# Head transposes two slots behind their mix, the gated product held to its place, and the pooling maps moved between the products

## The chip, the core and the metric

The kernel runs on one core of a Trainium2 chip. The metric is the device time of one execution in microseconds (us); lower is better. The engines are named as the profile names them: PE (TensorE) multiplies matrices, PEld is its weight load, DVE (VectorE) and ACT (ScalarE) and POOL (GpSimd) work on elements, SP (SyncE) issues the loads.

## What is computed

One block with 512 positions and 1024 channels, all in float32. Cut to what the change touches:

```python
hn = rms_norm(h, g_mix_pre)
z_sgu, z_conv, z_pool, z_gate = split(hn @ w_in)

# A) spatial gating: 8 heads of 128 channels, blocks of 128 positions
u, v = split(gelu(z_sgu)); v = layer_norm(v)
mixed = einsum('hij,bnjhc->bnihc', mask(w_s), v.reshape(blocks)) + b_s
br_a = (u * mixed) @ w_sgu_out

# C) pooling: four groups of 256 channels, windows 2, 4, 8, 16
for g, w in enumerate(windows):
    pooled[g] = trailing_mean(z_pool[g], w) - z_pool[g]
br_c = (einsum('bsgc,gcd->bsgd', pooled, w_pool) * s_pool) @ w_pool_out

merged = gate_a * br_a + gate_b * br_b + gate_c * br_c   # gates = sigmoid(z_gate)
h = h + rms_norm(merged @ w_out)
```

Branch B (a causal depthwise convolution of width 31, LayerNorm, swish), the feed-forward part and an embedding come beside and behind it; the change leaves them as they are.

## The kernel before

Activations lie transposed: channels on the 128 partitions, the 512 positions free, in eight tiles. A float32 product is three passes of a rounded type (high by high, high by low, low by high), so one tile of 128 outputs is 24 matmuls of 128 x 512. I call these 24 matmuls a **product**. Weights come in order of use: SP loads `raw`, ACT casts it to `hi`, DVE subtracts to get `lo`, two products ahead (`AHEAD = 2`).

A scheduler fixes the order of instructions on each engine when the program is built. Instructions issued inside `with order():` stay behind all those written before them on their engine. `drain(n)` issues n taps of the depthwise convolution (`acc` steps) on DVE, in order, behind each product.

In the **gating branch**, `natural` makes u with the positions on partitions, in two halves `c` of four slots `kk`, each of 24 matmuls into `ps_nat`. During the second half `mix_head(h)` splits v, multiplies it into `ps_mix` (3 matmuls), and DVE makes `gated[h]` from it and u. `turn_head(h)` transposes `gated[h]` into `ps_tr` (4 small matmuls), and ACT and DVE split the result into `sgu`. The loop turns head kk - 1 in slot kk and then mixes head kk; heads 3 to 7 follow behind the first gate products (`ps_gate`).

In the **pooling branch** eight products `ps_z` are copied by ACT to `z_all`, two for each of the groups 0 to 3. `pool_windows(g)` makes trailing sums of 2, 4, 8, 16 by doubling on POOL (`win`; 1 to 4 additions, each with a small copy), finishes them on DVE (`win` again), casts them on ACT to `pl_hi` and subtracts on DVE to `pl_lo`. `pool_map(g)` multiplies these by `w_pool` into `ps_pool` (12 matmuls), and ACT and DVE split the result into `pool`. The map of a group stands in the source behind the products of the next group; that of group 3 stands behind the third gate product (`POOL_LAG - 1` is 2).

`psum` has seven banks, handed out in turn, so a matmul into a new tile also waits until the bank's last reader is done. All engine instructions but POOL's carry L69, the line of a helper; what an instruction does is read from its tiles.

Of the kernel before, what the change touches and what calls it, by code (L numbers as in the profile page):

```python
# [13 lines left out]
ALU = mybir.AluOpType  # L14
# [7 lines left out]
NB = T // P  # L22
# [16 lines left out]

# The first GLU pairs are multiplied before the norm of x is known.  # L40
N_RAW = 3
N_FIRST = 2 * N_RAW * P
# Matrix products on nothing that raise the tensor engine's clock while the first loads run.
N_WARM = 8
# Taps of the depthwise convolution for each tile of GLU, v, gate a, pooling, gate c; and of u.
TAPS = (4, 3, 5, 3, 5)
TAPS_U = 4
# Where a norm or a piece of a residual goes between the products, counted in k-tiles.
STAT_K, STAT_A, STAT_H, STAT_F = 4, 2, 7, 2
# [5 lines left out]
class InOrder:  # L55
    """Engines whose instructions, while `on`, are issued behind all those written before them."""

# [24 lines left out]
def hybrid_block(  # L82
# [3 lines left out]
):  # L86
    """Activations live transposed (channels on partitions, the 512 positions free), so that every
    weight is a stationary operand as it lies in memory and is loaded once. A float32 product is
    three float32r passes: each operand is split exactly into a high and a low half of 12 bits."""
    nc = tc.nc  # L90
# [25 lines left out]

# [1 line left out]
    vec = const.tile([P, N_VEC + WIDTH * KT], F32, name="vec")  # L118
# [41 lines left out]

# [1 line left out]
    def split(hi, lo, src):  # L162
# [3 lines left out]
    def split_scaled(hi, lo, src, scale):  # L166
        """The halves of src * scale, scale one number per partition."""
        act_e.activation(out=hi, in_=src, func=AF.Copy, scale=scale)
        dve.scalar_tensor_tensor(out=lo, in0=src, scalar=scale, in1=hi,
                                       op0=ALU.mult, op1=ALU.subtract)  # L170
# [44 lines left out]
    def product(ps, w, acts, hs=FULL, k0=0, last=True):  # L215
        """ps[n, t] (+)= sum over the block's k of w[k, n] act[k, t]."""
        hi, lo = w
        for i, a in enumerate(acts):
            mm3(ps[:, hs], blk(hi, i), blk(lo, i), a[:, 0, hs], a[:, 1, hs],
                k0 + i == 0, last and i == len(acts) - 1)  # L220
# [7 lines left out]

# [1 line left out]
    background = []  # L230
# [6 lines left out]
    def rsqrt(y, a, t):  # L237
        """y = 1 / sqrt(a): a bit-pattern guess, a Newton step scaled by S, a third-order step."""
        dve.tensor_scalar(out=y.bitcast(I32), in0=a.bitcast(I32), scalar1=-0.5,
                          scalar2=RSQRT_SEED, op0=ALU.mult, op1=ALU.add)  # L240
        dve.tensor_tensor(out=t, in0=y, in1=y, op=ALU.mult)
        dve.scalar_tensor_tensor(out=t, in0=t, scalar=-RSQRT_C2 * RSQRT_S, in1=a,
                                 op0=ALU.mult, op1=ALU.mult)
        dve.scalar_tensor_tensor(out=y, in0=t, scalar=RSQRT_C1 * RSQRT_S, in1=y,
                                 op0=ALU.add, op1=ALU.mult)
        dve.tensor_tensor(out=t, in0=y, in1=y, op=ALU.mult)
        dve.tensor_tensor(out=t, in0=t, in1=a, op=ALU.mult)
        dve.scalar_tensor_tensor(out=t, in0=t, scalar=-10.0 / 3.0 * RSQRT_S ** 2, in1=t,
                                 op0=ALU.add, op1=ALU.mult)
        dve.scalar_tensor_tensor(out=y, in0=t, scalar=5.0 * RSQRT_S ** 4, in1=y,  # L250
                                 op0=ALU.add, op1=ALU.mult)

    def channel_mean(sums):
        """The mean over the channels of what `sums` holds by partition, on every partition."""
        ps = psum.tile([P, T], F32, tag="pst", name="ps_stat", bufs=1)
        ps = ps[:, :sums.shape[1]]
        pe.matmul(ps, lhsT=mean_mat, rhs=sums, start=True, stop=True)
        return ps

    def inv_rms(sums, y):  # L260
        """y = 1 / sqrt(mean over the channels + eps), on every partition; eps is in the sums."""
        rsqrt(y, channel_mean(sums), t2("rs_t", sums.shape[1]))
# [6 lines left out]
    def add_square(sums, src, i, engine):  # L269
        """The i-th of the squares that are summed; the second brings eps along."""  # L270
        if i == 0:
            act_e.activation(out=sums, in_=src, func=AF.Square)
        else:
            add_sq(sums, square(src), i, engine)
# [7 lines left out]

# [1 line left out]
    C_U, C_V, C_A, C_G, C_P, C_M = 0, 8, 16, 24, 32, 40  # L284
# [19 lines left out]
    for g in GROUPS:  # L304
        add_mix(C_P + 2 * g, C_P + 2 * g + 1)
        if g != GROUPS[0]:
            weights.add(w_pool[g - 1])
    POOL_LAG = 3
    for n in range(KT + POOL_LAG):
        if n < KT:  # L310
            add_mix(C_M + 16 + n)
        if n == POOL_LAG - 1:
            weights.add(w_pool[GROUPS[-1]])
        if n >= POOL_LAG:
            add_mix(S_POOL + n - POOL_LAG)
# [25 lines left out]

# [1 line left out]
    xg = [slot("br", f"xg{k}") for k in range(KT)]  # L343
# [15 lines left out]

# [1 line left out]
    h_conv = [slot("cv", f"h_conv{i}", F32) for i in range(4)]  # L361
# [67 lines left out]

# [1 line left out]
    def natural(dst, evacuate, taps):  # L431
        """dst[t, block, c] from z with the positions on partitions; yields behind each block."""
        for c in range(2):
# [69 lines left out]
    def mix_head(h):  # L503
        cs = slice(h * P, (h + 1) * P)
        vs = slot("tm", "v_split", shape=(2, NB, P))
        split(vs[:, 0], vs[:, 1], v_all[:, :, cs])
        ps = bank("ps_mix")
        mm3(ps, sg_hi[:, cs], sg_lo[:, cs], vs[:, 0], vs[:, 1], True, True)
        gated[h] = t2("gated")
        dve.scalar_tensor_tensor(  # L510
            out=gated[h].rearrange("p (n c) -> p n c", n=NB), in0=ps.rearrange("p (n c) -> p n c", n=NB),
            scalar=col("b_sgu_s", h), in1=u_all[:, :, cs], op0=ALU.add, op1=ALU.mult)

# [8 lines left out]
    for c, kk in natural(u_all, u_gelu, TAPS_U):  # L522
        if c == 1:
            if kk:
                turn_head(kk - 1)
            mix_head(kk)

# [1 line left out]
    merged = wide_tile("merged")  # L529
# [13 lines left out]
    for n in range(KT + SGU_LAG):  # L543
        if n < KT:
            gate_tile(merged[:, n, :], TAPS[2])
        if n < SGU_LAG:
            for h in ((3,), (4,), (5, 6), (7,))[n]:
                turn_head(h)
# [6 lines left out]

# [1 line left out]
    z_all = wide_tile("z_all")  # L557
# [34 lines left out]
    for g in GROUPS:  # L592
        for n in (2 * g, 2 * g + 1):
            ps = bank("ps_z")
            product(ps, weights.get(), hn)
            act_e.copy(z_all[:, n, :], ps)
            drain(TAPS[3])
        pool_windows(g)
        if g != GROUPS[0]:
            pool_map(g - 1)  # L600

    gates = []
    for n in range(KT + POOL_LAG):
        if n < KT:
            gates.append(t2("gate"))
            gate_tile(gates[n], TAPS[4])
        if n == POOL_LAG - 1:
            pool_map(GROUPS[-1])
        if n >= POOL_LAG:
# [5 lines left out]

# [1 line left out]
    drain(len(background))  # L617
# [31 lines left out]

    # ---- output projection, post-norm, residual; the last tiles a half of the positions at a time,  # L650
    # so that the norm of one half runs behind the product of the other ----
    o_all = wide_tile("o_all")
# [4 lines left out]
    class Residual:  # L657
        """h += o * y tile by tile, and the halves of h * scale; the low half runs a tile behind."""

# [49 lines left out]
    with order():  # L709
# [23 lines left out]

# [1 line left out]
        banks = [bank("ps_f") for _ in range(2 * N_PAIR)]  # L735
# [92 lines left out]
    with order():  # L828
# [26 lines left out]

# [1 line left out]
        w_ple_1 = weights.get(0)  # L857
# [31 lines left out]
def _blocks(w):  # L889
    """[K, N] -> [N / 128, 128, K]: one block for each 128 outputs, its k-tiles side by side."""  # L890
    k, n = w.shape
    return w.reshape(k // P, P, n // P, P).transpose(2, 1, 0, 3).reshape(n // P, P, k)


def _wide_blocks(w):
    """[1024, 1024] -> [8, 128, 1024]: for each half of the outputs, pairs of k-tiles."""
    return w.reshape(4, 2, P, 2, T).transpose(3, 0, 2, 1, 4).reshape(8, P, D)
# [54 lines left out]
```

## Time and profile before

| what | value |
|---|---|
| median of 3 runs | 987.28 us (987.15 to 988.0) |
| span of the profiled execution, first to last instruction | 984.9 us |
| so outside the span, by the median | about 2.4 us |
| PE busy | 974.1 us, 99% of the span |
| DVE busy | 675.5 us, 69% |
| ACT busy | 347.1 us, 35% |
| POOL busy | 87.4 us, 9% |
| granted TensorE clock | 1.000 over the span |

The profile is of one execution, whose own device time is not listed; the span is taken to lie 2.4 us below the median. In the timeline a row gives the start in us from the span's start, the duration, the engine, the operation with its tiles, the number of instructions merged into the row and, in brackets, how long the engine stood idle before it and whose end ended that. A DVE row ends about 0.09 us behind the start of the next, and a 128 x 512 matmul is listed with 0.39 us though the next starts 0.23 us after it. In the text a **step** is the time from one start to the next.

### The profile page before, as it was taken

The page shows a single profiled execution, that of the slowest core. Times are in us where ns is not written, and L with a number is a line of the kernel's source. Part 1 is how long each engine was busy: PE and PEld are TensorE (multiplying, and loading weights), DVE is VectorE, ACT ScalarE, POOL GpSimd, SP SyncE. Part 2 cuts the span into 40 slices and gives each one's busy share as a digit, 9 for nine tenths or more (in the row PEclk, how much of TensorE's full clock was granted, in tenths as well). Part 3 has the DMA queues.
Part 4 walks back from the last instruction along what each step waited for, and adds up shares of the span by engine and source line. Part 5 has one row for each costly group of instructions (what it writes and reads, how often), then busy time and mean ns, then how long its engine had stood idle before and what let it go on. Part 6 is the DMA issues. An engine that isn't in the chain of part 4 may idle for free.

```text
span 984.9 us, 11718 instructions
## 1 busy us (share of the span) xinstructions
PE 974.1 (99%) x4682; PEld 818.4 (83%) x4682; DVE 675.5 (69%) x903; ACT 347.1 (35%) x483; POOL 87.4 (9%) x64
## 2 busy tenths in 40 slices
PE   9999999899999999999999999999999999999998
PEld 6788888688888788888888998888888888888897
DVE  7998789998988799967556687554445442223675
ACT  6422333332223332246426443332232322223442
POOL 4000004000003702160000010000000000000000
PEclk9999999999999999999999999999999999999999
DMA  6433331322222232231328102323222333334312
GB/s 226 143 107 107 109 106 65 106 69 103 86 97 86 76 128 86 102 113 65 116 99 277 65 25 74 116 86 107 88 105 87 104 84 107 93 92 141 107 43 86
DMA packets 30006, 100.53 MB, mean 102 GB/s; under 512 B 3456, under 2 KB 3968, under 8 KB 29952
## 3 DMA queue, kind: packets, MB, share of 16 engines
q1 hardware_dynamic: 29808, 99.75, 30.2%
q8 instruction: 36, 0.59, 0.2%
q14 instruction: 18, 0.15, 0.0%
q10 hardware_dynamic: 144, 0.04, 0.0%
HBM read 97.68 MB, written 2.10 MB: 101 GB/s over the span
## 4 chain that ended last, share of the span: by engine, by line
PE 89%; DVE 7%; issue 2%; DMA 1%; ACT 1%; SPq 0%; DVEq 0%; ACTq 0%
PE ps_f L69 24%; PE ps_gate L69 13%; PE ps_br L69 13%; PE ps_fo L69 12%; PE ps_ag L69 5%; PE ps_pg L69 5%; PE ps_o L69 5%; PE ps_nat L69 4%; PE ps_z L69 4%; DVE lo L69 2%; DVE acc L69 1%; PE ps_pool L69 1%; PE ps_ple L69 1%; DVE v_all L69 1%; DMA first_all<-in_w_first 1%
## 5 line engine op out<-in xcount | busy, mean ns | idle before, releaser
L69 ACT CAST hi<-raw 128x1024 fp32r<-128x1024 f32 (+3 forms) x158 | 162.5, 1030 | 455.6 <-PE ps_br L69 88.4
L69 DVE TENSOR_TENSOR lo<-raw,hi 128x1024 fp32r<-128x1024 f32 (+3 forms) x158 | 201.4, 1276 | 107.5 <-ACT hi L69 106.8
L69 DVE SCALAR_TENSOR_TENSOR acc<-h_conv,vec,acc 128x511 f32<-128x511 f32 (+14 forms) x240 | 184.2, 768 | 5.1
L69 PE MATMUL ps_f<-hg,hi 128*128 128x512 f32 (+1 forms) x624 | 184.3, 378 | 0.0
L69 PEld LDWEIGHTS ps_f<-hg,hi 128*128 128x128 f32 x624 | 115.1, 188 | 21.7
L69 PE MATMUL ps_gate<-hn,hi 128*128 128x512 f32 x384 | 119.4, 392 | 0.0
L69 PE MATMUL ps_f<-hg,lo 128*128 128x512 f32 (+1 forms) x312 | 117.8, 378 | 0.0
L69 PE MATMUL ps_fo<-f,hi 128*128 128x512 f32 (+1 forms) x396 | 110.9, 366 | 0.0
L69 PEld LDWEIGHTS ps_gate<-hn,hi 128*128 128x128 f32 x384 | 72.0, 188 | 15.9 <-issue 1.0
L69 PEld LDWEIGHTS ps_fo<-f,hi 128*128 128x128 f32 x396 | 71.7, 189 | 12.2
L69 PE MATMUL ps_nat<-hi,hn 128*128 128x512 f32 x256 | 79.0, 389 | 0.0
L69 PE MATMUL ps_gate<-hn,lo 128*128 128x512 f32 x192 | 74.8, 389 | 0.0
L69 PE MATMUL ps_fo<-f,lo 128*128 128x512 f32 (+1 forms) x198 | 72.3, 365 | 0.0
L69 PEld LDWEIGHTS ps_f<-hg,lo 128*128 128x128 f32 x312 | 58.7, 188 | 11.0
L69 PEld LDWEIGHTS ps_nat<-hi,hn 128*128 128x128 f32 x256 | 48.1, 188 | 10.0
L69 DVE TENSOR_TENSOR f<-ps_f,h_inv 128x512 f32<-128x512 f32 x22 | 15.2, 689 | 56.5 <-PE ps_f L69 56.5
L69 PE MATMUL ps_nat<-lo,hn 128*128 128x512 f32 x128 | 49.8, 389 | 0.0
L69 PE MATMUL ps_ag<-hn,hi 128*128 128x512 f32 x160 | 49.5, 390 | 0.2 <-DVE sig L69 0.2
L69 PEld LDWEIGHTS ps_gate<-hn,lo 128*128 128x128 f32 x192 | 36.1, 188 | 7.6
L69 PEld LDWEIGHTS ps_fo<-f,lo 128*128 128x128 f32 x198 | 37.3, 189 | 6.0
L69 DVE TENSOR_TENSOR silu<-ps_f,h_inv 128x512 f32<-128x512 f32 x22 | 15.2, 690 | 36.0 <-PE ps_f L69 35.9
L69 PE MATMUL ps_br<-pool,hi 128*128 128x512 f32 x128 | 39.6, 389 | 0.0
(214 smaller groups left out, 1566.1 us busy)
## 6 DMA issues: line engine op xcount, KB each, us to landing
raw<-in_w_mix SPq DMA_DIRECT2D x90, 512.0 KB, 3.2
raw<-in_w_ffn_in SPq DMA_DIRECT2D x44, 512.0 KB, 3.2
raw<-in_w_ffn_out SPq DMA_DIRECT2D x16, 448.0 KB, 3.2
raw<-in_w_ffn_out SPq DMA_DIRECT2D x8, 512.0 KB, 3.5
raw<-in_w_ple_gate SPq DMA_DIRECT2D x8, 512.0 KB, 4.1
x_all<-in_xT SPq DMA_DIRECT2D x8, 256.0 KB, 6.6
h_all<-in_xT SPq DMA_DIRECT2D x4, 512.0 KB, 5.4
out_dram<-pg SPq DMA_DIRECT2D x7, 256.0 KB, 2.0
```

What stands on the lines that cost most here:

```text
L69: inst = op(*args, **kw)
```

## The change

Three things. In the gating branch, a head is turned two slots behind its mix: slot kk turns head kk - 2, and head 2 joins head 3 behind the first gate product. The `gated` step is put inside `with order():`, so it stands in DVE's queue where it is written. In the pooling branch `pool_map` moves: the maps of groups 0 and 1 stand behind the first product of the group after next, those of groups 2 and 3 behind the first and the second gate product. The list of weights follows.

```diff
     for g in GROUPS:
-        add_mix(C_P + 2 * g, C_P + 2 * g + 1)
-        if g != GROUPS[0]:
-            weights.add(w_pool[g - 1])
+        add_mix(C_P + 2 * g)
+        if g > 1:
+            weights.add(w_pool[g - 2])
+        add_mix(C_P + 2 * g + 1)
...
-        if n == POOL_LAG - 1:
-            weights.add(w_pool[GROUPS[-1]])
+        if n < 2:
+            weights.add(w_pool[2 + n])
...
-        dve.scalar_tensor_tensor(
-            out=gated[h].rearrange("p (n c) -> p n c", n=NB), in0=ps.rearrange("p (n c) -> p n c", n=NB),
-            scalar=col("b_sgu_s", h), in1=u_all[:, :, cs], op0=ALU.add, op1=ALU.mult)
+        with order():
+            dve.scalar_tensor_tensor(
+                out=gated[h].rearrange("p (n c) -> p n c", n=NB),
+                in0=ps.rearrange("p (n c) -> p n c", n=NB),
+                scalar=col("b_sgu_s", h), in1=u_all[:, :, cs], op0=ALU.add, op1=ALU.mult)
...
         if c == 1:
-            if kk:
-                turn_head(kk - 1)
+            if kk > 1:
+                turn_head(kk - 2)
             mix_head(kk)
...
-            for h in ((3,), (4,), (5, 6), (7,))[n]:
+            for h in ((2, 3), (4,), (5, 6), (7,))[n]:
                 turn_head(h)
...
             drain(TAPS[3])
+            if g > 1 and n == 2 * g:
+                pool_map(g - 2)
         pool_windows(g)
-        if g != GROUPS[0]:
-            pool_map(g - 1)
...
             gate_tile(gates[n], TAPS[4])
-        if n == POOL_LAG - 1:
-            pool_map(GROUPS[-1])
+        if n < 2:
+            pool_map(2 + n)
```

On PE, at the end of slot kk = 1 of u's second half (its matmuls read `hn_229` and `hn_230`, those of slot 2 `hn_231` onwards), there stood before:

```order
L69 MATMUL ps_nat<-hi,hn_230 128x512 x2
L69 MATMUL ps_nat<-lo,hn_230 128x512
L69 MATMUL ps_tr<-ident,gated 128x128 x4
L69 MATMUL ps_mix<-v_split,w_hi 128x512 x2
L69 MATMUL ps_mix<-v_split,w_lo 128x512
L69 MATMUL ps_nat<-hi,hn_231 128x512 x2
```

and now:

```order
L69 MATMUL ps_nat<-hi,hn_230 128x512 x2
L69 MATMUL ps_nat<-lo,hn_230 128x512
L69 MATMUL ps_mix<-v_split,w_hi 128x512 x2
L69 MATMUL ps_mix<-v_split,w_lo 128x512
L69 MATMUL ps_nat<-hi,hn_231 128x512 x2
```

The transpose of head 0 has gone to the end of slot 2, with the mix of head 2 behind it; those of heads 2 and 3 stand together behind the first gate product. On DVE the `gated` step of head 1 has gone ahead of a `lo` that it followed, and that of head 2 directly behind the next `lo`, ahead of an `sgu` step.

On DVE, between the low half of group 2 (`pl_lo`) and the finishing step of group 3 (`win<-win,z_all 128x2x496`), there stood before:

```order
L69 TENSOR_TENSOR pl_lo<-win,pl_hi 128x1024
L69 TENSOR_TENSOR lo<-raw,hi 128x1024
L69 SCALAR_TENSOR_TENSOR pool_2554<-ps_pool,vec,pool_2554 128x512
L69 TENSOR_TENSOR lo<-raw,hi 128x1024
L69 TENSOR_SCALAR acc_226<-h_conv_222,vec 128x512
L69 SCALAR_TENSOR_TENSOR pool_2564<-ps_pool,vec,pool_2564 128x512
L69 TENSOR_TENSOR lo<-raw,hi 128x512
L69 SCALAR_TENSOR_TENSOR acc_226<-h_conv_222,vec,acc_226 128x511
L69 SCALAR_TENSOR_TENSOR win<-win,z_all 128x2x496
```

and now, behind the same `pl_lo` and the same first `lo`:

```order
L69 TENSOR_SCALAR acc_226<-h_conv_222,vec 128x512
L69 SCALAR_TENSOR_TENSOR acc_226<-h_conv_222,vec,acc_226 128x511
L69 SCALAR_TENSOR_TENSOR acc_226<-h_conv_222,vec,acc_226 128x510
L69 SCALAR_TENSOR_TENSOR acc_226<-h_conv_222,vec,acc_226 128x509
L69 TENSOR_TENSOR lo<-raw,hi 128x512
L69 SCALAR_TENSOR_TENSOR acc_226<-h_conv_222,vec,acc_226 128x508
L69 SCALAR_TENSOR_TENSOR pool_2592<-ps_pool,vec,pool_2592 128x512
L69 TENSOR_TENSOR lo<-raw,hi 128x1024
L69 SCALAR_TENSOR_TENSOR acc_226<-h_conv_222,vec,acc_226 128x507
L69 SCALAR_TENSOR_TENSOR pool_2602<-ps_pool,vec,pool_2602 128x512
L69 SCALAR_TENSOR_TENSOR acc_226<-h_conv_222,vec,acc_226 128x506
L69 SCALAR_TENSOR_TENSOR win<-win,z_all 128x2x496
```

Five more `acc` steps stand ahead of group 3's `win`, and five stand ahead of the first step that waits for `ps_pool`, where there was none.

On ACT, from the copy of the last `ps_z` to the cast of group 3's `pl_hi`, there stood before (a `gate` row is the sigmoid behind a gate product; the third one follows the last row):

```order
L69 COPY z_all<-ps_z 128x512
L69 ACTIVATE pool_2554<-ps_pool,vec 128x512
L69 CAST hi<-raw 128x1024
L69 ACTIVATE pool_2564<-ps_pool,vec 128x512
L69 CAST hi<-raw 128x512
L69 ACTIVATE gate<-ps_gate 128x512
L69 CAST hi<-raw 128x1024
L69 ACTIVATE gate<-ps_gate 128x512
L69 CAST pl_hi<-win 128x1024
L69 CAST hi<-raw 128x1024
```

and now:

```order
L69 COPY z_all<-ps_z 128x512
L69 CAST hi<-raw 128x512
L69 ACTIVATE gate<-ps_gate 128x512
L69 ACTIVATE pool_2592<-ps_pool,vec 128x512
L69 CAST hi<-raw 128x1024
L69 ACTIVATE pool_2602<-ps_pool,vec 128x512
L69 CAST hi<-raw 128x1024
L69 ACTIVATE gate<-ps_gate 128x512
L69 CAST pl_hi<-win 128x1024
L69 CAST hi<-raw 128x1024
```

The cast of `pl_hi` stands behind the second gate's sigmoid in both. On PE the two matmuls `ps_pool<-pl_hi,hi` of group 3 stood directly behind the third gate product, and now directly behind the second.

## Rows read from the trace of the kernel before

**Rows 1.** The page's first part: busy time, share and instructions of each engine.

```profile
PE 974.1 (99%) x4682; PEld 818.4 (83%) x4682; DVE 675.5 (69%) x903; ACT 347.1 (35%) x483; POOL 87.4 (9%) x64
```

**Rows 2.** Waits of PE: what waited, for what, us in total, times, longest.

```profile
PE ps_tr L69 <- DVE gated L69: 3.2, 2, 1.6
...
PE ps_pool L69 <- ACT pl_hi L69: 1.0, 1, 1.0
```

**Rows 3.** Timeline of PE around the head transposes.

```profile
173.24 0.39 PE L69 MATMUL ps_nat<-lo,hn 128*128 128x512 f32 x1
175.19 0.66 PE L69 MATMUL ps_tr<-ident,gated 128*128 128x128 f32 x4 [1.56 <-DVE gated L69]
...
176.37 0.62 PE L69 MATMUL ps_nat<-hi,hn 128*128 128x512 f32 x2
...
190.18 0.66 PE L69 MATMUL ps_tr<-ident,gated 128*128 128x128 f32 x4 [1.59 <-DVE gated L69]
```

**Rows 4.** Timeline of DVE in the same stretch.

```profile
174.39 0.75 DVE L69 SCALAR_TENSOR_TENSOR gated<-ps_mix,vec,u_all 128x512 f32<-128x512 f32 x1
175.05 0.73 DVE L69 SCALAR_TENSOR_TENSOR acc<-h_conv,vec,acc 128x502 f32<-128x502 f32 x1
175.70 1.22 DVE L69 TENSOR_TENSOR lo<-raw,hi 128x1024 fp32r<-128x1024 f32 x1
176.84 0.69 DVE L69 TENSOR_TENSOR v_split<-v_all,v_split 128x512 fp32r<-128x512 f32 x1
177.44 3.06 DVE L69 SCALAR_TENSOR_TENSOR acc<-h_conv,vec,acc 128x501 f32<-128x501 f32 x4
180.41 1.22 DVE L69 TENSOR_TENSOR lo<-raw,hi 128x1024 fp32r<-128x1024 f32 x1
181.55 0.75 DVE L69 SCALAR_TENSOR_TENSOR gated<-ps_mix,vec,u_all 128x512 f32<-128x512 f32 x1
```

**Rows 5.** Timeline of PE around the maps of groups 2 and 3.

```profile
332.27 0.39 PE L69 MATMUL ps_z<-hn,lo 128*128 128x512 f32 x1
333.62 0.73 PE L69 MATMUL ps_pool<-pl_hi,hi 128*128 128x512 f32 x2 [0.97 <-ACT pl_hi L69]
...
352.80 0.62 PE L69 MATMUL ps_pool<-pl_hi,hi 128*128 128x512 f32 x2
```

**Rows 6.** Timeline of ACT in that stretch.

```profile
332.52 1.04 ACT L69 CAST pl_hi<-win 128x1024 fp32r<-128x1024 f32 x1 [3.96 <-DVE win L69]
333.47 1.04 ACT L69 CAST hi<-raw 128x1024 fp32r<-128x1024 f32 x1
334.42 0.58 ACT L69 COPY z_all<-ps_z 128x512 f32<-128x512 f32 x1
...
348.29 0.59 ACT L69 ACTIVATE gate<-ps_gate 128x512 f32<-128x512 f32 x1
350.27 1.05 ACT L69 CAST pl_hi<-win 128x1024 fp32r<-128x1024 f32 x1 [1.39 <-DVE win L69]
```

**Rows 7.** Timeline of DVE in that stretch.

```profile
333.60 1.93 DVE L69 TENSOR_TENSOR pl_lo<-win,pl_hi 128x1024 fp32r<-128x1024 f32 x1 [0.52 <-ACT pl_hi L69]
335.46 2.91 DVE L69 TENSOR_TENSOR lo<-raw,hi 128x1024 fp32r<-128x1024 f32 x1
341.26 0.75 DVE L69 SCALAR_TENSOR_TENSOR pool<-ps_pool,vec,pool 128x512 fp32r<-128x512 f32 x1 [2.89 <-ACT pool L69]
...
348.13 1.18 DVE L69 SCALAR_TENSOR_TENSOR win<-win,z_all 128x992 f32<-128x992 f32 x1
```

**Rows 8.** Timeline of POOL in that stretch: two additions of group 3.

```profile
338.49 1.89 POOL L567 TENSOR_TENSOR win<-win 128x1020 f32<-128x1020 f32 x1
...
342.69 3.32 POOL L567 TENSOR_TENSOR win<-win 128x1008 f32<-128x1008 f32 x1
```

**Rows 9.** Timeline of PE: its first row.

```profile
1.33 3.60 PE L69 MATMUL ps_warm<-warm_up 128*128 128x512 bf16 x8 [1.33 <-DVE warm_up L69]
```

**Rows 10.** The page's part on DMA issues: KB each, us to landing.

```profile
raw<-in_w_mix SPq DMA_DIRECT2D x90, 512.0 KB, 3.2
```

## Prediction

> **What bounds the kernel now.** The page's first part comes first: TensorE is busy for 974.1 us, 99% of the span, VectorE for 675.5 [rows 1]. A change that leaves the matmuls as they are can win only what TensorE waits, and lose by making it wait. So the view of PE's waits is next: head transposes waited for `gated` twice, 3.2 us, and a pooling map once for `pl_hi`, 1.0 [rows 2]. The timeline of PE says where: 1.56 at 175.19 and 1.59 at 190.18 [rows 3], 0.97 at 333.62 [rows 5]. A matmul counts there for 0.39 while the next starts 0.23 behind it, so each wait costs 0.16 more than its bracket: 1.72, 1.75 and 1.13, together 4.6. That is all the change can remove. The timeline of DVE shows why `gated` is late: VectorE has no gap between 174.39 and 181.55, taps and weight halves stand around the step [rows 4].
>
> **The gating branch.** I walk on with steps of VectorE: `gated` 0.66, `acc` 0.65, `lo` 1.14, `v_split` 0.60 (`sgu` has its shape), four `acc` 2.97 [rows 4]. Up to `gated` of head 0 (174.39, done 175.14) nothing differs. TensorE ends slot 1 at 173.47 [rows 3], and now goes on with a mix (3 x 0.23 = 0.68) and slot 2 (24 x 0.227 = 5.44): 179.59. Head 0's transposes find their input done, so the 1.72 goes. Transposes and mix take 1.18 (175.19 to 176.37) [rows 3], slot 3 runs from 180.77 to 186.21, transposes and mix to 187.39.
>
> The first gate product takes the bank of head 2's mix, so it waits for `gated` of head 2. VectorE: from 180.41 `gated` 0.66, `lo` 1.14, `acc` 0.65, `v_split` 0.60, four `acc` 2.97, `lo` 1.14 bring 187.57, and 0.75 more its end, 188.32. TensorE waits for about **0.95**, new, and ends the gate product at about 193.8. Head 2's transposes follow (0.4), then head 3's, whose `gated` stands behind `sgu` 0.60, `acc` 0.65, `v_split` 0.60, three `acc` 2.2, `lo` 1.14 and `acc` 0.65 after the previous one: 188.23 + 5.84 = 194.07, done 194.82. TensorE is there at 194.2 and waits for **0.6**, new. The 1.75 at 190.18 is gone. Behind VectorE's queue stand the same splits as before, and its work is the same, only in another order. Sum: -1.72 - 1.75 + 0.95 + 0.6, **-1.9**. Bounds: -3.5 if neither new wait comes, 0 if VectorE's queue runs 2 late.
>
> The view of PE's waits names nothing else between 191 and 332 [rows 2], so I carry the 1.9 to the last `ps_z`: it ends at 332.50 [rows 5] and now at 330.6.
>
> **The pooling maps.** Maps 0 and 1 move behind one more product and were not waited for: 0. Map 2 goes behind the first gate product, 5.44 later, while it was 1.13 late: **-1.1**, with over 4 to spare. The four loads of `w_pool` move by one or two places in SP's queue. A load lands in 3.2 [rows 10] and is issued two products, 10.9, ahead, so I take 0; without that cover it would be at most 3.2.
>
> Map 3 moves the other way. It stood behind the third gate product and now stands behind the second, one gate product earlier. Before, its matmuls started at 352.80, and `pl_hi` had been done at 351.32 [rows 5, 6]: 1.5 of slack. Now TensorE comes to it two gate products and one map (12 x 0.227 = 2.72) behind the last `ps_z`: 330.6 + 5.44 + 2.72 + 5.44 = 344.2. What it needs: `pl_hi` of group 2 on ACT (332.52), behind it in ACT's queue a `hi` and the copy of the last `ps_z` (334.42), four additions on POOL, `win` on VectorE (348.13), `pl_hi` of group 3 (350.27, done 351.32) [rows 6, 7]. If that chain moves ahead by the 1.9 and keeps its length, it ends at 349.4, and the new wait is **5.2**.
>
> I expect it longer. The rows show that VectorE and POOL stop each other: the `lo` at 335.46 took 2.91 where the same step takes 1.22, and the POOL addition at 342.69 took 3.32 where 338.49's took 1.89 [rows 4, 7, 8]. In the kernel before, POOL had a free stretch, because VectorE stood idle for 2.89 until 341.26, waiting for map 2's `ps_pool` [rows 7]. The order now has five `acc` steps in that place. VectorE's own work from `pl_lo` of group 2 to `win` of group 3 is `pl_lo` and two `lo` 3 x 1.14, seven `acc` steps 7 x 0.65, a short `lo` 0.60 and two `pool` 2 x 0.66: 9.9. POOL's is four additions with their copies, two of which took 338.49 to 342.69, so 8.4 [rows 8]. In full turns, with only `pool` beside POOL (its source is in PSUM, and I take that as free): 9.9 - 1.3 + 8.4 = 17.0, where it was 348.13 - 333.60 = 14.5 [rows 7]. That lengthens the chain by 2.4, and the wait to **7.6**. Ends: 2.5 if the two never meet, since ACT still has to do a `hi` (0.95), the second gate's sigmoid (0.5) and `pl_hi` (1.05) behind that gate product [rows 6]; 9.1 if group 2's three additions are stretched too, which delays the copy that starts group 3. I take 7.6, as the order leaves VectorE no gap.
>
> The Trainium skill, page "SBUF — State Buffer", section "Who interferes with whom", has a rule for this: a VectorE instruction with two SBUF inputs and a GpSimd instruction that reads SBUF exclude each other, and the one that comes later blocks for the other's whole length. This trace agrees with it (2.91 against 1.22). By that rule the wait is the 7.6; by the busy times alone it would be 2.5.
>
> **After the stall.** TensorE would stand idle longer than anywhere in this trace, where 1.6 is the longest [rows 2] and no slower matmuls follow. At its start, after idling, eight matmuls took 3.60 [rows 9], 0.45 each where 0.227 is usual, so at the lower of its two clocks, 1.2 GHz (the granted clock reads 1.000 over the span, so I go by the matmuls). Bounds: 0, as after 1.6, and 1.8 (8 x 0.22), as at the start; twice that if it lasts longer. A wait of 7.6 is nearer to the start than to 1.6, so I take **+1.8**.
>
> The Trainium skill, page "TensorE: Matmul & The Clock Gate", section "Part 1: The HAM clock gate (the "warmup" mystery)", says that an idle array falls to 1.2 GHz and that sustained work brings 2.4 back. The trace shows the second half at its start; no wait in it is long enough for the first.
>
> **The sum.** -1.9 - 1.1 + 7.6 + 1.8 = +6.4. The span of 984.9 becomes 991.3; what lies outside it (2.4) stays, so the median of 987.28 becomes **993.7**.
>
> **Rivals.**
> 1. *The chain keeps its length.* Wait 5.2, for which speaks that the chain before had turns too; against it, the order without the idle 2.89. 987.28 - 3.0 + 5.2 = 989.5, and 991.3 with the slow matmuls.
> 2. *No turns.* Only ACT's order holds, wait 2.5: 986.8, no change to be told. Against it speak the 2.91 and 3.32.
> 3. *Faster: map 3 is not waited for.* The place is the same, the price of the wait 0, the total 984.3. It decides where the chain from the last `ps_z` to `pl_hi` shrinks from 18.8 (332.50 to 351.32) to under 14.6, so that less than 1.0 of wait stands against the 3.0 won. Against it: the sigmoid ahead of `pl_hi` on ACT waits for the second gate product, which alone costs 2.5.
> 4. *Worse:* all three effects at their ends, wait 9.1 and slow matmuls for twice as long: 987.28 - 3.0 + 9.1 + 3.6 = 997.0.
>
> **How the numbers follow.** A measurement here can tell 0.2%, 2.0 us, from no change. The forecast (turns, with or without slow matmuls, 992 to 995.5) has 0.55, rival 1 0.20, rival 2 0.12, rival 3 0.06, rival 4 0.07. Rivals 2 and 3 and part of 4 are left out: 988.5 to 996.5. Within the forecast alone it is 992 to 995.5. Faster (below 985.3) 0.06; same (985.3 to 989.3) 0.15, rival 2 and the lower edge of rival 1; slower 0.79.
>
> **What would show it.** In the changed profile: no wait at the transposes of head 0 and at the end of slot 3; a wait of about 1 at the first `ps_gate` and of 0.6 at head 3's `ps_tr`, both for `gated`; none at map 2; one of 7 to 8 at `ps_pool` for `pl_hi` around 344, with POOL's four additions stretched beyond 11 us and no idle on VectorE among them; then matmuls 0.45 apart. A wait near 5 there says rival 1, near 2.5 rival 2. The prediction is wrong if map 3 is reached late or its cast comes early, and if the two new waits for `gated` are as long as those they replace.

## The result and the profile after

The changed kernel takes 994.23 us (median of 4 runs, 993.77 to 996.14), the kernel before 987.21: ratio 1.0072, 95% interval 1.0058 to 1.0086, so 7.0 us slower. 993.7 was forecast, in 988.5 to 996.5. The profiled execution has a span of 992.4, 7.5 more than before.

The waits of PE after the change (what waited, for what, us in total, times, longest), the answer to [rows 2]:

```profile
PE ps_pool L69 <- ACT pl_hi L69: 7.9, 1, 7.9
...
PE ps_gate L69 <- DVE gated L69: 0.9, 1, 0.9
...
PE ps_tr L69 <- DVE gated L69: 0.4, 1, 0.4
```

The two waits of 1.6 at `ps_tr` are gone, and two shorter ones stand in their place. At `ps_pool` one wait of 7.9 stands where 1.0 stood. The timeline of PE has the places, as [rows 3] and [rows 5] had them before:

```profile
179.78 0.60 PE L69 MATMUL ps_tr<-ident,gated 128*128 128x128 f32 x4
...
188.54 0.73 PE L69 MATMUL ps_gate<-hn,hi 128*128 128x512 f32 x2 [0.86 <-DVE gated L69]
...
195.08 0.63 PE L69 MATMUL ps_tr<-ident,gated 128*128 128x128 f32 x4 [0.36 <-DVE gated L69]
...
352.42 1.22 PE L69 MATMUL ps_pool<-pl_hi,hi 128*128 128x512 f32 x2 [7.91 <-ACT pl_hi L69]
353.44 1.05 PE L69 MATMUL ps_gate<-hn,hi 128*128 128x512 f32 x2
354.29 0.63 PE L69 MATMUL ps_gate<-hn,lo 128*128 128x512 f32 x1
```

Head 0 is transposed without a wait, the first gate product waits for head 2's bank, head 3's transposes wait for their `gated`. The large wait is that of map 3. Behind it two matmuls of a gate take 1.05, where 0.62 is usual [rows 3]; from start to start that is 0.43 for each (353.44 to 354.29).

Why `pl_hi` came so late is read on ACT, POOL and VectorE. ACT, against [rows 6]:

```profile
331.75 1.05 ACT L69 CAST pl_hi<-win 128x1024 fp32r<-128x1024 f32 x1 [5.22 <-DVE win L69]
...
333.65 0.58 ACT L69 COPY z_all<-ps_z 128x512 f32<-128x512 f32 x1
...
345.27 0.59 ACT L69 ACTIVATE gate<-ps_gate 128x512 f32<-128x512 f32 x1
351.32 1.04 ACT L69 CAST pl_hi<-win 128x1024 fp32r<-128x1024 f32 x1 [5.46 <-DVE win L69]
```

The cast of group 3 starts at 351.32, behind 5.46 of idle that ended with `win`; the sigmoid ahead of it had been done since 345.86. So ACT's order, the floor of 2.5, was not what held it. VectorE, against [rows 7]:

```profile
332.84 1.23 DVE L69 TENSOR_TENSOR pl_lo<-win,pl_hi 128x1024 fp32r<-128x1024 f32 x1 [1.20 <-ACT pl_hi L69]
...
335.11 2.12 DVE L69 TENSOR_SCALAR acc<-h_conv,vec 128x512 f32<-128x512 f32 x1
337.26 3.83 DVE L69 SCALAR_TENSOR_TENSOR acc<-h_conv,vec,acc 128x511 f32<-128x511 f32 x3
341.01 2.37 DVE L69 TENSOR_TENSOR lo<-raw,hi 128x512 fp32r<-128x512 f32 x1
...
344.63 2.67 DVE L69 TENSOR_TENSOR lo<-raw,hi 128x1024 fp32r<-128x1024 f32 x1
...
349.19 1.18 DVE L69 SCALAR_TENSOR_TENSOR win<-win,z_all 128x992 f32<-128x992 f32 x1
```

and POOL, against [rows 8]:

```profile
334.31 2.63 POOL L570 TENSOR_TENSOR win<-z_all 128x1022 f32<-128x1022 f32 x1 [1.38 <-ACT z_all L69]
...
337.35 2.41 POOL L570 TENSOR_TENSOR win<-win 128x1020 f32<-128x1020 f32 x1
...
340.44 2.40 POOL L570 TENSOR_TENSOR win<-win 128x1016 f32<-128x1016 f32 x1
...
343.51 2.70 POOL L570 TENSOR_TENSOR win<-win 128x1008 f32<-128x1008 f32 x1
346.16 1.19 POOL L571 COPY win<-win 128x16 f32<-128x16 f32 x1
```

The first addition of group 3 and the copy behind the last one were, before the change:

```profile
335.08 2.20 POOL L567 TENSOR_TENSOR win<-z_all 128x1022 f32<-128x1022 f32 x1 [0.63 <-ACT z_all L69]
...
345.95 0.39 POOL L568 COPY win<-win 128x16 f32<-128x16 f32 x1
```

VectorE has no idle between 332.84 and 349.19, and four of the rows shown are far over their bare length: a `lo` of 1.22 takes 2.67, three taps 3.83 for 2.2. The rows not shown there keep theirs. POOL's additions, 1.89 each when alone [rows 8], take 2.40 to 2.70. From `pl_lo` of group 2 to `win` of group 3 it is 16.35, where it was 14.53. Nearly all of these 1.8 lies on POOL: from its first addition to the end of its last copy it takes 13.04, and 11.26 before.

The windows around the stall (length, busy time of PE, PEld, DVE, ACT, POOL, then the granted clock, the share of the DMA engines and GB/s):

```profile
343.00:346.00 3.00, 1.51 (x7) 0.93 (x5) 3.00 (x4) 1.54 (x2) 2.92 (x2) 1.00 0.51 152
346.00:350.00 4.00, 0.00 (x0) 0.00 (x0) 4.00 (x5) 0.00 (x0) 1.36 (x2) 0.64 0.41 147
350.00:352.00 2.00, 0.00 (x0) 0.00 (x0) 2.00 (x5) 0.68 (x1) 0.00 (x0) 0.50 0.01 2
352.00:354.00 2.00, 1.58 (x4) 1.29 (x5) 2.00 (x3) 0.37 (x1) 0.00 (x0) 0.50 0.35 92
354.00:356.00 2.00, 2.00 (x7) 1.52 (x6) 0.81 (x2) 0.00 (x0) 0.00 (x0) 0.50 0.45 174
356.00:358.00 2.00, 2.00 (x7) 1.61 (x6) 0.00 (x0) 0.00 (x0) 0.00 (x0) 0.65 0.01 4
358.00:360.00 2.00, 2.00 (x10) 1.65 (x9) 0.00 (x0) 0.00 (x0) 0.00 (x0) 1.00 0.00 0
```

The granted clock falls to 0.50 (1.2 GHz) while PE idles and is back at 1.00 (2.4 GHz) from 358. In between the windows count 7 matmuls of PE in 2 us, and 10 from 358.

To put each change of time in its place, I cut every profile at three starts on PE: the first `ps_nat`, the first `ps_br` that reads `sgu`, and the first `ps_o` that reads `mix` at full width. The gating branch lies in the second column, the pooling branch in the third.

| kernel | first `ps_nat` at | to first `ps_br` | to first `ps_o` | to the end | span |
|---|---|---|---|---|---|
| before | 96.1 | 127.6 | 291.4 | 469.8 | 984.9 |
| the change | 96.3 | 125.6 | 300.7 | 469.8 | 992.4 |
| gating branch alone | 96.9 | 125.6 | 291.3 | 469.9 | 983.7 |
| pooling branch alone | 96.8 | 127.6 | 301.1 | 469.8 | 995.3 |
| map 3 behind the third gate | 97.7 | 125.6 | 293.7 | 469.8 | 986.8 |
| map 3 behind the fourth gate | 96.5 | 125.5 | 291.2 | 469.8 | 983.0 |
| stall filled | 96.6 | 125.5 | 298.4 | 469.8 | 990.3 |
| taps behind the map | 96.6 | 125.6 | 297.5 | 469.8 | 989.5 |
| gating alone, fewer taps | 96.1 | 123.8 | 291.4 | 469.8 | 981.1 |
| the best version | 97.0 | 123.8 | 290.6 | 469.8 | 981.2 |

The change wins 2.0 in the gating branch and loses 9.3 in the pooling branch. The first column moves by up to 1.6 between executions; that is the start, which no kernel here changes.

### The profile page after: what moved, and what is told of

Same layout as the page of the kernel before. It is cut to its first block, busy times and chain, and to the rows that moved or that the text cites. A ratio compares the mean times of both kernels' runs of the same rounds, so it can differ in the third digit from the quotient of the medians.

```text
span 992.4 us, 11720 instructions
## 1 busy us (share of the span) xinstructions
PE 976.7 (98%) x4682; PEld 820.5 (83%) x4682; DVE 682.1 (69%) x903; ACT 346.8 (35%) x483; POOL 91.0 (9%) x64
## 4 chain that ended last, share of the span: by engine, by line
PE 88%; DVE 7%; ACT 2%; issue 1%; DMA 1%; SPq 0%; DVEq 0%; ACTq 0%
PE ps_f L69 24%; PE ps_br L69 13%; PE ps_fo L69 12%; PE ps_gate L69 12%; PE ps_nat L69 6%; PE ps_ag L69 5%; PE ps_pg L69 5%; PE ps_o L69 5%; PE ps_z L69 4%; DVE lo L69 2%; DVE acc L69 1%; PE ps_ple L69 1%; PE ps_pool L69 1%; DVE v_all L69 1%; DMA x_all<-in_xT 1%
## 5 line engine op out<-in xcount | busy, mean ns | idle before, releaser
L69 DVE TENSOR_TENSOR lo<-raw,hi 128x1024 fp32r<-128x1024 f32 (+3 forms) x158 | 204.5, 1295 | 112.9 <-ACT hi L69 112.5
L69 DVE SCALAR_TENSOR_TENSOR acc<-h_conv,vec,acc 128x511 f32<-128x511 f32 (+14 forms) x240 | 190.1, 792 | 5.1
L69 PE MATMUL ps_br<-sgu,hi 128*128 128x512 f32 x128 | 39.4, 389 | 0.0
```

Source lines behind the costliest of these rows:

```text
L69: inst = op(*args, **kw)
```

## The experiments

My theory: map 3 comes one gate product too early for a chain (group 2's cast, the copy behind it, POOL, VectorE, the cast) that the same edit has lengthened, since taps now stand where POOL ran free; and the idle time lowers TensorE's clock. Rivals: the gating edit brings TensorE there too early; the place of the map alone, with a chain no longer than before; another cause for the slow matmuls.

**Gating branch alone.** The pooling hunks of the diff are left out.

> Only the gating branch is changed (transposes two slots behind, gated held to its place); the pooling branch is as before. My theory: the two waits of 1.72 and 1.75 go, two new ones of about 1.0 and 0.5 come, so -1.9 us: about 985.3, ratio 0.998. Rival: the new waits are as long as the old, ratio 1.000.

984.92, ratio 0.9974 (0.9964 to 0.9984). The waits of PE:

```profile
PE ps_pool L69 <- ACT pl_hi L69: 1.0, 1, 1.0
PE ps_gate L69 <- DVE gated L69: 0.9, 1, 0.9
...
PE ps_tr L69 <- DVE gated L69: 0.4, 1, 0.4
```

The new waits are shorter than the old, and the stage is 2.0 shorter. Map 2's wait of 1.0 stays, since that is the pooling edit's. Of the three parts of the change one did nothing: with the `with order():` around `gated` taken out, the order on all five engines is the same row by row.

**Pooling branch alone.** The gating hunks are left out.

> Only the pooling branch is changed; the gating branch is as before. My theory: the chain to the last group's pl_hi starts from the pooling products, so it moves with TensorE, and the wait stays at 7.9 whatever the gating branch does; with the wait of 1.1 at map 2 gone and 2.4 for slow matmuls: 987.2 - 1.1 + 8.1 + 2.4 = 996.6, ratio 1.0095. Rival: TensorE only comes too early because the gating edit has moved it up by 1.9; then the wait is 6.0 and the time about 992.7.

996.55, ratio 1.0090 (1.0076 to 1.0104), and PE's waits are

```profile
PE ps_pool L69 <- ACT pl_hi L69: 7.9, 1, 7.9
PE ps_tr L69 <- DVE gated L69: 3.2, 2, 1.6
```

The wait is the same 7.9 without the gating edit. That rival falls: the chain starts from products of TensorE, and moves with it. What the gating branch wins it keeps.

**Map 3 behind the third gate product again.**

```diff
+    POOL_AT = {0: 2, 2: 3}
...
-        if n < 2:
-            pool_map(2 + n)
+        if n in POOL_AT:
+            pool_map(POOL_AT[n])
```

> The whole change, but the map of group 3 stands again behind the third gate product. My theory: TensorE comes 5.44 later, at about 349.8, and the chain, long from its turns with VectorE, still ends at about 352.4: a wait of 2.6 in place of 7.9, no slow matmuls, total 987.2 - 1.9 - 1.1 + 2.7 = 986.9, ratio 0.9997. Rival (the chain is no longer than before the change, its place alone is wrong): no wait, 984.2, ratio 0.997.

988.96, ratio 1.0017 (1.0008 to 1.0026). PE at map 3:

```profile
354.55 0.74 PE L69 MATMUL ps_pool<-pl_hi,hi 128*128 128x512 f32 x2 [3.23 <-ACT pl_hi L69]
```

A wait of 3.2 stands at the place where the map had 1.5 of slack before the change. So the place is not all: the chain itself is longer. It is even longer than in the change, 17.11 from `pl_lo` to `win` (334.21 to 351.32), with one more `acc` step ahead of `win`; its 0.65 is about what the wait has over the 2.6 expected. Of the 1.7 above the kernel before, the table accounts for 0.3 (-2.0 and +2.3). The rest I did not settle. The profiled execution lies 1.6 later at its first `ps_nat` and shows a clock of 0.71 between 40 and 45 us, behind an early wait of 2.1. Each of the eleven runs lists a mean clock of 0.996 to 0.998, of the kernel before only 3 of 24 runs do; whether the other runs lose their time there or behind the 3.2, no trace here says.

**Map 3 behind the fourth gate product.** The same with `{0: 2, 3: 3}`.

> The whole change, but the map of group 3 stands behind the fourth gate product, directly ahead of the first branch product that reads it. My theory: TensorE comes at about 355.2, the chain ends at 352.4, no wait for pl_hi, total 984.2, ratio 0.997. Rival: the branch product then waits for the last two tiles of the pooled branch, split on ACT and VectorE after the map, 1 to 2 us, and the time is 985 to 986.

984.87, ratio 0.9977 (0.9968 to 0.9985): no better than the gating branch alone. `pl_hi` is not waited for, but the branch product behind it is cut up with gate matmuls. PE, then VectorE:

```profile
363.30 0.50 PE L69 MATMUL ps_gate<-hn,lo 128*128 128x512 f32 x1 [0.26 <-DVE lo L69]
...
364.11 0.39 PE L69 MATMUL ps_gate<-hn,lo 128*128 128x512 f32 x1
364.61 0.50 PE L69 MATMUL ps_br<-pool,hi 128*128 128x512 f32 x1
```

```profile
358.30 3.82 DVE L69 SCALAR_TENSOR_TENSOR acc<-h_conv,vec,acc 128x499 f32<-128x499 f32 x5
362.03 1.22 DVE L69 TENSOR_TENSOR lo<-raw,hi 128x1024 fp32r<-128x1024 f32 x1
363.17 0.72 DVE L69 SCALAR_TENSOR_TENSOR acc<-h_conv,vec,acc 128x494 f32<-128x494 f32 x1
363.81 0.74 DVE L69 SCALAR_TENSOR_TENSOR pool<-ps_pool,vec,pool 128x512 fp32r<-128x512 f32 x1
```

ACT has made its halves of `pool` by 359.66, and VectorE begins the first of the others at 363.81, behind taps. The `ps_br` that stands behind that `pool` step starts at 364.61, 0.27 later than usual. The rival was right in kind, not in size: a late `pool` takes the place of the late `pl_hi`, but the time lies just below its 985 to 986. The stage is 291.2, and with map 2's wait gone it should be 290.3; the wait for `lo` (0.42 with its tail) and the 0.27 make up 0.7 of the 0.9, and the rest is open.

**The stall filled with matmuls on nothing.** The kernel does 30 more matmuls, and its outputs do not read them.

```diff
+        if n == 1:
+            fill = psum.tile([P, T], F32, tag="pst", name="ps_fill", bufs=1)
+            with order():
+                for _ in range(N_FILL):
+                    pe.matmul(fill, lhsT=warm_up[:, :P], rhs=warm_up, start=True, stop=True)
         if n < 2:
             pool_map(2 + n)
```

> The whole change, and between the second gate product and the map of group 3 thirty 128x512 matmuls on nothing, into a bank that nothing reads; they take 30 x 0.227 = 6.8 us of the 7.9 that TensorE waits there. My theory: the wait ends at the same place, but TensorE has not idled for long, so its clock stays up and the third gate product is not slow: 2.4 less, 994.2 - 2.4 = 991.8, ratio 1.0047. Rival: the matmuls behind the stall are slow for another cause (weights or halves that come late), 994.2, ratio 1.007.

992.05, ratio 1.0047 (1.0035 to 1.0060). PE:

```profile
344.55 6.65 PE L70 MATMUL ps_fill<-warm_up 128*128 128x512 bf16 x30
...
352.64 0.73 PE L70 MATMUL ps_pool<-pl_hi,hi 128*128 128x512 f32 x2 [1.44 <-ACT pl_hi L70]
```

`pl_hi` comes as late as ever, but the granted clock is 1.00 in every window from 340 to 370, and the pooling stage is 2.3 shorter (298.4). That is the price of the idle time beyond the idle time itself, shown by taking it away with work that is of no use.

**Taps behind the map.** No `acc` step stands ahead of map 2's `pool` on VectorE.

```diff
-            gate_tile(gates[n], TAPS[4])
+            gate_tile(gates[n], 0)
         if n < 2:
             pool_map(2 + n)
+        if n < KT:
+            drain(TAPS[4])
```

> The whole change, but the taps of each gate product are issued behind the map that follows it, so that no acc step stands on VectorE ahead of the first step that waits for ps_pool, as in the kernel before. My theory: POOL runs free in that gap again, the stretch from pl_lo of group 2 to win of group 3 is 14.5 as before in place of 16.35, the wait for pl_hi falls from 7.9 to about 6.1 and the time to 992.3, ratio 1.005. Rival: the length of the chain is set by POOL and ACT alone, whatever taps stand there: wait 7.9, 994.2, ratio 1.007.

991.27, ratio 1.0041 (1.0029 to 1.0054), more than I expected of it. VectorE, then POOL, then PE:

```profile
333.10 1.23 DVE L69 TENSOR_TENSOR pl_lo<-win,pl_hi 128x1024 fp32r<-128x1024 f32 x1 [1.20 <-ACT pl_hi L69]
...
339.18 0.75 DVE L69 SCALAR_TENSOR_TENSOR pool<-ps_pool,vec,pool 128x512 fp32r<-128x512 f32 x1 [1.37 <-ACT pool L69]
...
346.46 1.19 DVE L69 SCALAR_TENSOR_TENSOR win<-win,z_all 128x992 f32<-128x992 f32 x1
```

```profile
334.57 2.64 POOL L570 TENSOR_TENSOR win<-z_all 128x1022 f32<-128x1022 f32 x1 [1.38 <-ACT z_all L69]
...
345.41 0.40 POOL L571 COPY win<-win 128x16 f32<-128x16 f32 x1
```

```profile
349.69 1.22 PE L69 MATMUL ps_pool<-pl_hi,hi 128*128 128x512 f32 x2 [4.92 <-ACT pl_hi L69]
```

From `pl_lo` to `win` it is 13.36 in place of 16.35, and the wait falls by the same 3.0, to 4.9. The taps are the same in number and only stand later; so it was they that had stretched the chain, in two ways. POOL needs 11.24 from its first addition to the end of its last copy, as before the change, where it needed 13.04: 1.8 of the 3.0 are turns with POOL. And `win` follows 0.65 behind that copy, where it stood 1.84 behind it: the other 1.2 are taps and other steps in VectorE's own queue. The rest, 4.9, is the price of the place.

**Gating alone with fewer taps.**

```diff
-TAPS_U = 4
+TAPS_U = (4, 3)
...
-                drain(taps)
+                drain(taps[c])
...
-            gate_tile(merged[:, n, :], TAPS[2])
+            gate_tile(merged[:, n, :], TAPS[2] + (n >= 4))
```

> Only the gating branch is changed, and in the second half of u each slot issues three taps in place of four; the four taps are given back beside the last four gate products of that branch. My theory: the two new waits (0.9 and 0.4, with 0.16 each) come from VectorE's full queue alone and vanish: 984.9 - 1.6 = 983.3, ratio 0.996. Rival: the taps cost the same where they are given back, 984.9, ratio 0.9975.

984.15, ratio 0.9969 (0.9956 to 0.9981). Both new waits are gone from PE's list, and the gating stage is 123.8 in place of 125.6, 1.8 shorter; the stage behind it is as long as before, so the four taps cost nothing where they went. The runs scatter from 982.93 to 985.21, and the median shows only 0.8 of it; why they scatter is not shown.

**The best version.** The gating branch of the last run; of the pooling edit only map 2's move, with the taps behind it (`POOL_AT = {0: 2, 2: 3}`, maps 0 and 1 as before the change).

> The gating branch as in the run with fewer taps; in the pooling branch only the map of group 2 is moved, behind the first gate product, with the taps of that product behind the map; the map of group 3 stands behind the third gate product as before the change. My theory: the wait of 1.1 at map 2 goes and map 3, which had 1.5 of slack, is not waited for: 983.3 - 1.1 = 982.2, ratio 0.995. Rival: the chain of group 3 becomes longer by more than its slack, and a wait of about 1 at map 3 takes the gain: 983.3, ratio 0.996.

983.29, ratio 0.9958 (0.9945 to 0.9970), the lowest median of all, though its interval overlaps that of the run before it. PE:

```profile
349.03 0.73 PE L69 MATMUL ps_pool<-pl_hi,hi 128*128 128x512 f32 x2 [0.22 <-ACT pl_hi L69]
```

That wait of 0.2 is all that is left of the pooling branch's: 290.6 in place of 291.4.

## Why the prediction was right

Direction, place and mechanism held, and the forecast time was 0.5 short. By its terms, in us of the profiled span:

| term | predicted | measured |
|---|---|---|
| heads 0 and 2 no longer waited for | -1.72, -1.75 | the same, both gone |
| first gate product waits for head 2 | +0.95 | +1.02 (0.86 and 0.16) |
| head 3's transposes | +0.6 | +0.52 (0.36 and 0.16) |
| map 2 | -1.1 | -1.1, gone |
| map 3 waits for `pl_hi` | +7.6 | +8.07 (7.91 and 0.16) |
| slow matmuls behind it | +1.8 | +2.3 (the filled stall) |
| sum | +6.4 | +7.3; the span moved by 7.5 |

The terms fall 0.9 short of what was measured, the slow matmuls and map 3 by about 0.5 each.

The walk with VectorE's steps in the gating branch came out to 0.1, because VectorE has no gap there: where an engine's queue is full, a new order of the same work can be added up row by row.

The term of map 3 has two parts that erred in opposite ways. I left group 2 at no delay: its cast should have moved ahead by 1.9, from 332.52 [rows 6] to 330.6, and came at 331.75, 1.1 late. I had named that as the upper end (1.5), for the reason that the traces show: group 2's three additions with their copies took 9.64 on POOL, where they took 8.12 before. And I took full turns, 17.0, where 16.35 was measured: some of the steps do lie beside each other. So part of the closeness is luck. Before, the same stretch was 14.5 [rows 7]; of the 16.35 the taps' share is the 3.0 that the run with the taps behind the map gave back, and only 1.8 of it are turns with POOL.

Of the rivals, the one with a chain of unchanged length (5.2) is close to what that run shows, 4.9, once the taps are moved, but there two differences cancel: the stretch is 1.2 shorter than before the change, and group 2's cast still comes late. In the change itself that rival falls. "No turns" (2.5) falls with the sigmoid done 5.5 ahead of the cast. The rule that the Trainium skill gives on the page "SBUF — State Buffer", section "Who interferes with whom", agrees with all three timelines: two-input steps of VectorE and POOL's additions take their turns, and the `pool` steps, with one source in PSUM, keep their length of 0.74 to 0.75 in the midst of them. I had overlooked a step with one wide input: the first tap, a `TENSOR_SCALAR`, takes 2.12 beside POOL, and 0.55 elsewhere in the same trace, so steps with two inputs are not the only ones that take turns.

```profile
203.21 0.55 DVE L69 TENSOR_SCALAR acc<-h_conv,vec 128x512 f32<-128x512 f32 x1
```

The slow matmuls were sized from the kernel's start (1.8) and cost 2.3: the lower clock lasted from the end of the stall, 352.4, to about 357.5, longer than eight matmuls. The page "TensorE: Matmul & The Clock Gate" of the Trainium skill, section "Part 1: The HAM clock gate (the "warmup" mystery)", says that an idle array falls to 1.2 GHz; the granted clock of 0.50 in the windows from 350 to 356 agrees.

One step was loose: 2.4 outside the span. The runs list span and time of each execution, and they differ by about 1.8 throughout; the execution profiled before was simply 0.6 below the median. That is why the time is off by only 0.5 where the span is off by 1.1 (991.3 against 992.4): this too is luck.

## What to carry to other kernels

When work is moved on the engine that bounds, check each piece's own deadline: three maps were moved later, one quietly came a product earlier, and it brought most of the loss. Background work that is issued "behind each product" belongs to the chain that runs beside it: moving a consumer past a product also moves the taps in front of its producer, and on VectorE beside POOL they take longer than alone (three took 3.83 in place of 2.2). And a stall on TensorE can cost more than its length, as those of 4.9 and 7.9 did here, so a forecast for one needs a term for the matmuls behind it.

## What the runs showed of the hardware

The clock did not fall at every wait. Behind 3.2 us of idle, in the run with map 3 behind the third gate, two matmuls took 0.74, as after short waits; behind 4.9 they took 1.22, as behind 7.9. Yet in the run with map 3 behind the third gate a wait of only 2.1, at the first `ps_ag` (until 41.84), was followed by a granted clock of 0.50 from 43 to 45, so the length of the wait alone does not tell. At the start the same kernel order reaches full speed at different times: between 6 and 8 us the kernel before made five matmuls, and the run with map 3 behind the fourth gate ten. What is won there is waited for again at the first `ps_ag` (1.6 in that run), so it hardly shows in the span; the first `ps_nat` lies at 96.1 in the kernel before and at 96.5 in that run. It comes latest, at 97.7, in the run whose clock fell behind the wait of 2.1. The granted clock reads 1.00 through the slow start, though it follows the later fall closely.
